# A two-layer hybrid-attention trunk on one core: projections in another order, roped tiles rounded later and a head at a time, one PSUM bank moved from projections to scores

## The chip, the cores and the metric

The kernel runs on one core of a Trainium2 chip. The metric is device time in microseconds for one launch; of the kernel before there are three timed runs, and one further execution was taken by the hardware profiler. Engine names are those of the profile: PE is TensorE, PEld its weight load, DVE VectorE, ACT ScalarE, POOL GpSimd, SP the queue that issues the DMAs.

## The reference

Two layers on `x` (1 x 512 x 1024, f32). Each layer has a mixer of three attention groups on one common projection, and a gated MLP with a causal depthwise convolution:

```python
for l in range(DEPTH):                       # 2
    h = rms_norm(x, attn_pre_norm[l])
    x = x + rms_norm(hybrid_mixer(h, ...), attn_post_norm[l])
    h = rms_norm(x, ffn_pre_norm[l])
    x = x + rms_norm(conv_ffn(h, ...), ffn_post_norm[l])
# hybrid_mixer: proj = h @ w_in, split into
(fq, fk, fv, ff, nq, kc, vc, ks, vs, kw, vw, ng, dq, dk, dv)
# o_fox: 4 heads, causal softmax with forget gates    (fq, fk, fv, ff)
# o_nsa: 8 heads in 2 groups, three branches summed with gates ng:
#        compressed (kc, vc), selected (ks, vs), sliding window (kw, vw)
# o_dil: 4 heads, dilated windows                      (dq, dk, dv)
# rope on nq, kc, ks, kw, dq, dk;   mix = concat(o_fox, o_nsa, o_dil) @ w_out
```

All matrices are f32. The kernel computes each product from parts in a rounded format: a value is rounded (its high part), the difference is rounded again (its low part), and high x high, high x low and low x high are summed.

## The kernel before, in words

A layer goes through these stages: the norm and its transposes, the projections fk, fv and fq, the *mixer* with all remaining projections, the end of the out projection, the norm, the up projection with convolution and gate, the down projection. The mixer of layer 0 lies at about 60 to 345 us of the span, that of layer 1 about 696 us later.

The mixer is a software pipeline of 96 *units*: one unit is one head, one branch and one of four query tiles of 128 rows (forget heads: units 0 to 15; NSA heads with the selected and the window branch: 16 to 79; dilated heads: 80 to 95). One unit starts in each *slot* of the loop, and `LAGS` says how many slots later its further stages follow: scores on PE (`st_scores`, lag 0), mask and maximum on DVE (`st_max`, 1), exponential on ACT (`st_exp`, 1), reciprocal on DVE and scaling on POOL (`st_norm`, 2), transposes on PE (`st_turn`, 4), rounding of the transposed tile on ACT and DVE (`st_keep_hi`, `st_keep_lo`, 5), products with v on PE (`st_values`, 7), evacuation (`st_out`, 7).

Between the slots `main_pieces` supplies the projections, cut into *steps* of about 1.4 us of PE: first five steps, then 1.4 steps in each of twelve slots, 0.8 after that. A projection of 128 columns (`projT`) takes four steps and ends in one PSUM bank of the pool `acc`; sv and dv (`proj256`) take eight steps and two banks. After its last step `keep` follows: the rope (`rope`: shuffle and cosine product on DVE, sine product and sum on POOL), and one step later `keep2`, the rounding of the roped tile, both heads of 64 rows in a row, in `q_evac` or `k_evac` (high part on ACT, low part on DVE; for k each of them twice, once for each half of the partitions). Before a unit's scores, `operands` looks whether its q, k and v are there; where not, `until` runs steps back to back until they are:

```python
def until(key, n=1):
    while len(store.get(key, ())) < n and (live[0] or pieces.late):
        step()
```

On PE this order of calls is the order of the program (`tc.manual_schedule`). On DVE, ACT and POOL a scheduler orders the instructions by their dependences and priorities. A list `plan` holds the weights in the order in which SP loads them; each is split into a high part (ACT, line 144) and a low part (POOL, line 148, for the names in `ONPOOL`; DVE, line 152, for others).

PSUM has eight banks, shared out by `PSB`: three for projections (`acc`), two for scores (`s`), two for transposes (`pt`), one for the products with v (`o`). A tile of a pool waits until the readers of the tile that had its bank are done. The compressed branch (`c_scores`, `c_norm`, `c_turn`, `c_keep`) runs beside units 47 to 57; its tiles are taken from the pool named by `CT`.

Of the kernel before, what the change touches and what calls it, by code (L numbers as in the profile page):

```python
# [13 lines left out]
ALU = mybir.AluOpType  # L14
# [11 lines left out]
NBIG = 24  # L26
NROW = 10
LAGS = (1, 2, 4, 5, 7, 7)
TAIL = 4
ONPOOL = ("sv", "dv", "dq", "dk", "ks", "nq0", "kw", "kc", "nq1",  # L30
          (0, "fk", 0), (0, "fk", 1), ("up", 0, 1), ("up", 0, 2), ("up", 0, 3), ("up", 1, 0))
# [3 lines left out]
CL = (1, 3, 5, 6)  # L35
OT = (("acc", "acc"), ("acc", "s"), ("s", "o"), ("acc", "acc"))
PCUT = ((0, 2), (2, 4))
X8 = "acc"
CT = "acc"
FIRST = 5  # L40
DCUTS = ("w1", "wo")
EV = (1, 3, 1, 1)
ORDER = (0, 1, 2, 4, 3, 5, 6, 7, 8)
# [29 lines left out]
def tile_hybrid_block(  # L73
# [15 lines left out]
    dram = ctx.enter_context(tc.tile_pool(name="dram", bufs=1, space=bass.MemoryType.DRAM))  # L89
    PSB = {"acc": 3, "o": 1, "s": 2, "pt": 2}  # L90
    uid = [0]
# [5 lines left out]
    def ps(tag):  # L97
        return psum.tile([128, 512], F32, tag=tag, bufs=PSB[tag], name=nm(tag))

    def bt(shape, dt=F32, name="b"):  # L100
        return big.tile(shape, dt, tag="b", name=nm(name))
# [7 lines left out]
    def f(ap):  # L109
        return ap.bitcast(F32)  # L110
# [50 lines left out]
    for l in range(DEPTH):  # L161
# [7 lines left out]
        def turned(name, *starts, spare=False):  # L169
            for c, c0 in enumerate(starts):  # L170
                plan.append(((l, name, c), [(wi[:, :, c0:c0 + 128], 0, 0)], 8, 128, spare))
# [6 lines left out]
        turned("kc", C_KC, C_KC + 128)  # L178
        turned("ks", C_KC + 256)
        for c in range(2):  # L180
            ks = slice(4 * c, 4 * c + 4)
            plan.append(((l, "sv", c), [(wi[:, ks, C_KC + 384:C_KC + 512], 0, 0), (wi[:, ks, C_KW + 128:C_KW + 256], 0, 128)],
                         4, 256, False))
        turned("nq0", C_NQ, C_NQ + 128)
        for kv, starts in enumerate(((C_KW,), (C_NQ + 256, C_NQ + 384))):
            for c in range(2):
                if c < len(starts):
                    plan.append(((l, ("kw", "nq1")[kv], c), [(wi[:, :, starts[c]:starts[c] + 128], 0, 0)], 8, 128, False))
                for d in range(2):
                    k0 = 8 * c + 4 * d  # L190
                    plan.append(((l, "w1", kv, 2 * c + d), [(w1s[kv][:, k0:k0 + 4, :], 0, 0)], 4, 256, False))
# [247 lines left out]
    for l in range(DEPTH):  # L439
# [21 lines left out]
        def rope(p):  # L461
# [6 lines left out]
            return r  # L468

        def q_evac(p):  # L470
            q = bt([128, 2, 512], F32R, "q")
            for j in range(2):
                src = p[64 * j:64 * j + 64, :]
                nc.scalar.activation(q[0:64, j, :], src, AF.Copy, scale=-0.125)
                nc.vector.scalar_tensor_tensor(q[64:128, j, :], src, -0.125, f(q[0:64, j, :]),  # L475
                                               op0=ALU.mult, op1=ALU.subtract)
            return q

        def k_evac(p):

            ks = []
            for j in range(2):
                k = bt([128, 2, 512], F32R, "k")
                src = p[64 * j:64 * j + 64, :]
                for u in (j, 1 - j):
                    nc.scalar.activation(k[64 * u:64 * u + 64, 0, :], src, AF.Copy)
                for u in (j, 1 - j):
                    nc.vector.tensor_sub(k[64 * u:64 * u + 64, 1, :], src, f(k[64 * j:64 * j + 64, 0, :]))  # L488
                ks.append(k)
            return ks  # L490
# [20 lines left out]
        wv = [getw(l, "fv", c, ahead=1) for c in range(3)]  # L511
        pk_ = [ps("acc"), ps("acc")]
        fv = [new_v(), new_v()]
# [205 lines left out]
        def keep(p, key):  # L719
            pieces.later(EV[3], keep2, rope(p), key)  # L720

        def keep2(r, key):
            store.setdefault(key, []).extend([q_evac(r)] if key[-1] == "q" else k_evac(r))

# [16 lines left out]
        def main_pieces():  # L741
# [69 lines left out]
            yield from projT("kc", turn=(win_k, win_v))  # L811
            yield from projT("ks", "nks")
            yield from proj256("sv", sv_evac, [])
            yield from projT("nq0", "nq")
            xc = rt((128, 256))
            for kv, g in ((0, projT("kw", "nkw")), (1, projT("nq1", "nq"))):
                while len(wins.get(kv, ())) < 2:
                    yield
                yield from merge(g, hidden(kv))
# [22 lines left out]
            yield from out_first()  # L842
            yield from out_start()

        def merge(a, b):
# [343 lines left out]
        with tc.manual_schedule(engines={mybir.EngineType.PE}):  # L1189
# [44 lines left out]
            table(AF.Silu, hs[3][:, 0:1])  # L1234
            pts = [ps(t) for t in ("acc", "acc", "s", "s")]
            for half in range(2):
# [17 lines left out]
        for i in range(11):  # L1254
            gt = bt([128, 2, 512], name="g")
            gts.append(gt)
            tg = ("acc", "acc", "s", "s") if i % 2 == 0 else ("pt", "pt", X8, "o")
            for c in range(2):
# [13 lines left out]

        dacc = [(ps("acc"), ps("acc")), (ps("s"), ps("s")), (ps("o"), ps(X8)), (ps("pt"), ps("pt"))]
        NK = DFF // 128
# [70 lines left out]
```

## Time and profile before

| | |
|---|---|
| timed runs, median (lowest to highest) | 1412.58 us (1411.82 to 1418.45) |
| profiled execution | 1416.81 us |
| its span (first to last instruction) | 1415.0 us, mean granted PE clock 0.986 |
| PE busy | 1337.1 us, 94% |
| DVE busy | 892.9 us, 63% |
| ACT busy | 725.6 us, 51% |
| POOL busy | 377.6 us, 27% |

A row of a timeline gives the start and the duration of an instruction (or of a run of equal ones, x count), its engine, line, operation, what it writes and reads, and in brackets how long the engine stood idle before it and which instruction ended that. The granted clock is a share of full speed; the two levels are 1.2 and 2.4 GHz, so that a mean between 0.5 and 1 is a stretch with both.

### The profile page before, as it was taken

How to read it: one execution, taken by the hardware profiler on the slowest of the kernel's cores; microseconds unless marked ns; L12 is line 12 of the kernel's file. 1: busy time of each engine (PE TensorE's matmuls, PEld its weight loads, DVE VectorE, ACT ScalarE, POOL GpSimd, SP SyncE). 2: the span in 40 equal slices, each digit the busy share in tenths (PEclk: the TensorE clock that was granted, in tenths of full speed). 3: DMA queues.
4: the chain of work that ended last, by engine and by line, in shares of the span. 5: the costliest groups of instructions: out<-in, count | busy, mean ns of one | idle time of the engine just before them, and what ended most of it. 6: DMA issues, size and time to landing. Idle time of an engine off the chain costs nothing.

```text
span 1415.0 us, 19975 instructions
## 1 busy us (share of the span) xinstructions
PE 1337.1 (94%) x7291; PEld 1151.2 (81%) x7291; DVE 892.9 (63%) x1867; ACT 725.6 (51%) x1469; POOL 377.6 (27%) x409
## 2 busy tenths in 40 slices
PE   6987999998999999999999988989989999999997
PEld 5876887887888888888887878979878888888886
DVE  7767878877655555533476687787686555554334
ACT  5656675775543333332374667677754333333322
POOL 2385576545000000000006657654440000000000
PEclk9999999999999999999999989999999999999999
DMA  6222321123233333323423132202313333323231
GB/s 175 76 60 75 99 71 31 46 75 119 66 99 96 98 96 98 96 98 111 119 90 90 60 105 75 60 31 69 112 60 89 91 103 91 103 91 104 90 120 59
DMA packets 161962, 123.67 MB, mean 87 GB/s; under 512 B 8329, under 2 KB 152137, under 8 KB 161865
## 3 DMA queue, kind: packets, MB, share of 16 engines
q1 hardware_dynamic: 161864, 122.40, 28.8%
q8 instruction: 57, 0.93, 0.3%
q14 instruction: 41, 0.33, 0.1%
HBM read 118.19 MB, written 4.19 MB: 86 GB/s over the span
## 4 chain that ended last, share of the span: by engine, by line
PE 70%; DVE 12%; ACT 7%; POOL 6%; issue 3%; DMA 1%; SPq 0%; POOLq 0%; DVEq 0%; ACTq 0%
PE acc L113 31%; PE s L113 16%; PE pt L113 12%; PE o L113 9%; PE pt L1107 2%; DVE k L488 1%; POOL r L467 1%; DVE q L475 1%; DVE wl_w L152 1%; POOL r L466 1%; ACT r L1089 1%; POOL wt L781 1%; DVE x L308 1%; DVE hl L274 1%; DVE pl L1129 1%
## 5 line engine op out<-in xcount | busy, mean ns | idle before, releaser
L152 DVE TENSOR_TENSOR wl_up<-raw_up,wh_up 128x1024 fp32r<-128x1024 f32 x78 | 95.5, 1225 | 163.2 <-ACT wh_up L144 163.2
L144 ACT ACTIVATE wh_up<-raw_up 128x1024 fp32r<-128x1024 f32 (+1 forms) x90 | 89.4, 1002 | 154.1 <-PE acc L113 67.9
L152 DVE TENSOR_TENSOR wl_wd<-raw_wd,wh_wd 128x1024 fp32r<-128x1024 f32 x42 | 51.5, 1225 | 133.5 <-ACT wh_wd L144 133.5
L113 PE MATMUL s<-k,q 128*128 128x512 f32 (+3 forms) x384 | 100.6, 343 | 23.8 <-DVE sm L1084 8.3
L148 POOL TENSOR_TENSOR wl_kc<-raw_kc,wh_kc 128x512 fp32r<-128x512 f32 x8 | 12.2, 1546 | 411.1 <-ACT wh_kc L144 411.1
L144 ACT ACTIVATE wh_wd<-raw_wd 128x1024 fp32r<-128x1024 f32 x42 | 44.5, 1060 | 144.5 <-PE pt L113 135.5
L1089 ACT ACTIVATE r<-r,sm 128x128 f32<-128x128 f32 x192 | 106.8, 557 | 19.7 <-DVE sm L1084 18.8
L1096 POOL TENSOR_SCALAR r<-r,sm,gates 128x128 f32<-128x128 f32 (+3 forms) x128 | 86.2, 680 | 88.0 <-DVE sm L1094 48.1
L113 PE MATMUL acc<-hh,wh_up 128*128 128x512 f32 (+1 forms) x272 | 102.4, 376 | 0.0
L113 PE MATMUL acc<-hl,wh_up 128*128 128x512 f32 (+1 forms) x272 | 102.4, 376 | 0.0
L113 PE MATMUL acc<-hh,wl_up 128*128 128x512 f32 (+1 forms) x272 | 102.4, 376 | 0.0
L113 PEld LDWEIGHTS s<-k,q 128*128 128x128 f32 x384 | 65.0, 198 | 36.0 <-DVE sm L1084 11.8
L1129 DVE TENSOR_TENSOR pl<-pt,ph 128x384 fp32r<-128x384 f32 x144 | 85.2, 593 | 13.0 <-ACT ph L1124 11.9
L1124 ACT ACTIVATE ph<-pt 128x384 fp32r<-128x384 f32 x144 | 74.4, 518 | 34.9 <-PE pt L1107 33.8
L1107 PE MATMUL pt<-ident,r 128*128 128x128 f32 x480 | 80.1, 283 | 7.7 <-POOL r L1096 4.9
L1084 DVE CUSTOM_DVE_ANT_0 r<-s,cmask 128x128 f32<-128x128 f32 (+3 forms) x160 | 74.8, 481 | 17.4 <-PE s L113 15.3
L113 PE MATMUL acc<-wh_wd,gh 128*128 128x512 f32 x252 | 83.7, 389 | 0.0
L113 PE MATMUL s<-hh,wh_up 128*128 128x512 f32 (+1 forms) x224 | 80.6, 360 | 0.9 <-DVE hl L274 0.9
L113 PE MATMUL s<-hl,wh_up 128*128 128x512 f32 (+1 forms) x224 | 80.3, 359 | 0.0
L113 PE MATMUL s<-hh,wl_up 128*128 128x512 f32 (+1 forms) x224 | 80.3, 359 | 0.0
L113 PE MATMUL o<-ph,v 128*128 128x256 f32 (+1 forms) x288 | 72.8, 279 | 0.8 <-DVE mx L1165 0.8
L113 PE MATMUL o<-pl,v 128*128 128x256 f32 (+1 forms) x288 | 70.0, 290 | 1.7 <-DVE pl L1129 1.7
(434 smaller groups left out, 4023.4 us busy)
## 6 DMA issues: line engine op xcount, KB each, us to landing
raw_up<-in_w_up_dram SPq DMA_DIRECT2D x88, 512.0 KB, 3.8
raw_wd<-in_w_down_dram SPq DMA_DIRECT2D x44, 512.0 KB, 3.4
raw_wo<-in_w_out_dram SPq DMA_DIRECT2D x16, 512.0 KB, 3.5
x<-in_x_dram SPq DMA_DIRECT2D x8, 512.0 KB, 5.7
raw_nq<-in_w_in_dram SPq DMA_DIRECT2D x8, 512.0 KB, 3.8
raw_w<-in_cmp_w_k_dram SPq DMA_DIRECT2D x8, 512.0 KB, 4.0
raw_w<-in_cmp_w_v_dram SPq DMA_DIRECT2D x8, 512.0 KB, 3.8
raw_fk<-in_w_in_dram SPq DMA_DIRECT2D x4, 512.0 KB, 4.8
```

What stands on the lines that cost most here:

```text
L113: nc.tensor.matmul(o, lhsT=lhsT, rhs=rhs, start=start, stop=stop, skip_group_check=True)
L144: nc.scalar.activation(hi[:, ks], raw[:, ks], AF.Copy)
L152: nc.vector.tensor_sub(lo[:, ks], raw[:, ks], f(hi)[:, ks])
L274: nc.vector.scalar_tensor_tensor(lo, src, gain[:, k:k + 1], f(hi), op0=ALU.mult, op1=ALU.subtract)
L308: nc.vector.scalar_tensor_tensor(xs[s][:, cs], hs[s][:, cs], stats["r", s // 2][:, j:j + 1], xs[s][:, cs], op0=ALU.mult, op1=ALU.add)
L466: nc.gpsimd.tensor_mul(w, w, sinT)
L1084: nc.vector.tensor_tensor_reduce(row[:, 0:n], u["S"][:, 0:n], u["mask"][:, 512 - n:512], op0=ALU.add, op1=ALU.min, scale=1.0, scalar=3.0e3 ...
L1089: nc.scalar.activation(row[:, 0:n], row[:, 0:n], AF.Exp, scale=-1.0, bias=sm_[:, 0:1], accum_out=sm_[:, 1:2])
L1096: nc.gpsimd.tensor_scalar(row[:, 0:n], row[:, 0:n], sm_[:, 2:3], g_, op0=ALU.mult, op1=ALU.mult)
L1107: nc.tensor.transpose(p[:, 128 * b:128 * b + 128], src, ident)
L1124: nc.scalar.activation(hi, src, AF.Copy)
L1129: nc.vector.tensor_sub(*u["lo"])
```

## The change

1. The order of the projections in `main_pieces`, and of the loads in `plan`. Before: kc, ks, sv, nq0 (two column groups), then kw merged with the first hidden layer of the compressed k, nq1 (two groups) merged with that of the compressed v, dv, dq, dk. After: kc, ks, nq0 (one group: heads 0 to 3's first 128 columns), kw, sv, then nq1 merged with the first hidden layer, nq2 and nq3 merged with the second, dv, dq, dk. The names nq0 to nq3 now stand for one group of 128 columns each.
2. `keep` does the rope at once, as before; the rounding of the two heads of a tile is now in two calls, two and three steps after the rope (`EV[3]` 1 to 2), instead of one call one step after it.
3. `PSB`: `acc` from three banks to two, `s` from two to three. Tiles that go from `acc` to `s`: the second of the two fk tiles, those of the compressed branch (`CT`), one of the out projection (`OT`), and one each in the transposes of the second norm, the up and the down projection.
4. `NROW` from 10 to 12: two more tiles of 128x512 f32 for rows.

The arithmetic is the same.

```diff
-NROW = 10
+NROW = 12
-ONPOOL = ("sv", "dv", "dq", "dk", "ks", "nq0", "kw", "kc", "nq1",
+ONPOOL = ("sv", "dv", "dq", "dk", "ks", "nq0", "kw", "kc", "nq1", "nq2", "nq3",
-OT = (("acc", "acc"), ("acc", "s"), ("s", "o"), ("acc", "acc"))
+OT = (("acc", "acc"), ("s", "s"), ("s", "o"), ("acc", "acc"))
-CT = "acc"
+CT = "s"
-EV = (1, 3, 1, 1)
+EV = (1, 3, 1, 2)
-    PSB = {"acc": 3, "o": 1, "s": 2, "pt": 2}
+    PSB = {"acc": 2, "o": 1, "s": 3, "pt": 2}
...
-        pk_ = [ps("acc"), ps("acc")]
+        pk_ = [ps("acc"), ps("s")]
...
         def keep(p, key):
-            pieces.later(EV[3], keep2, rope(p), key)
-
-        def keep2(r, key):
-            store.setdefault(key, []).extend([q_evac(r)] if key[-1] == "q" else k_evac(r))
+            r = rope(p)
+            if key[-1] == "q":
+                q = bt([128, 2, 512], F32R, "q")
+                pieces.later(EV[3], q_half, q, r, 0)
+                pieces.later(EV[3] + 1, last_q, key, q, r)
+            else:
+                pieces.later(EV[3], one_k, key, r, 0)
+                pieces.later(EV[3] + 1, one_k, key, r, 1)
+
+        def last_q(key, q, r):
+            q_half(q, r, 1)
+            store.setdefault(key, []).append(q)
+
+        def one_k(key, r, j):
+            k = bt([128, 2, 512], F32R, "k")
+            k_half(k, r, j)
+            store.setdefault(key, []).append(k)
...
             yield from projT("ks", "nks")
+            yield from projT("nq0", "nq")
+            yield from projT("kw", "nkw")
             yield from proj256("sv", sv_evac, [])
-            yield from projT("nq0", "nq")
             xc = rt((128, 256))
-            for kv, g in ((0, projT("kw", "nkw")), (1, projT("nq1", "nq"))):
+            for kv, g in ((0, projT("nq1", "nq")), (1, both(projT("nq2", "nq"), projT("nq3", "nq")))):
...
-            pts = [ps(t) for t in ("acc", "acc", "s", "s")]
+            pts = [ps(t) for t in ("acc", "s", "s", "s")]
...
-            tg = ("acc", "acc", "s", "s") if i % 2 == 0 else ("pt", "pt", X8, "o")
+            tg = ("acc", "s", "s", "s") if i % 2 == 0 else ("pt", "pt", X8, "o")
...
-        dacc = [(ps("acc"), ps("acc")), (ps("s"), ps("s")), (ps("o"), ps(X8)), (ps("pt"), ps("pt"))]
+        dacc = [(ps("acc"), ps("acc")), (ps("s"), ps("s")), (ps("o"), ps("s")), (ps("pt"), ps("pt"))]
```

`q_half` and `k_half` hold the loop bodies of the former `q_evac` and `k_evac`.

How the change moves instructions is seen at three places of layer 0. The first is PE ahead of the first score of slot 20, the first one that reads the window branch's k (`k_1577`); `acc_1510` is the compressed branch's first hidden layer with its weights `wh_w`, `wl_w`. Before:

```order
L113 MATMUL acc_1510<-wh_w_0_2_274_1541,wth_949 128x256 [waits Activation_49]
L113 MATMUL acc_1510<-wl_w_0_2_275_1542,wth_949 128x256 [waits DVE_49]
L113 MATMUL acc_1510<-wh_w_0_2_274_1541,wth_949 128x256
L113 MATMUL acc_1510<-wl_w_0_2_275_1542,wth_949 128x256
L113 MATMUL s_1587<-k_1577,q_1385 128x128 [waits Activation_49]
L113 MATMUL s_1587<-k_1577,q_1385 128x128 [waits DVE_49]
```

After, the same score (`k_1271` is now the window branch's k), and what stands before it:

```order
L113 MATMUL acc_1423<-hh_98,wh_nq_0_240_1346 128x512
L113 MATMUL acc_1423<-hl_102,wh_nq_0_240_1346 128x512
L113 MATMUL acc_1423<-hh_98,wl_nq_0_241_1347 128x512
L113 MATMUL s_1544<-k_1271,q_1104 128x128 x2
L113 MATMUL o_1555<-ph_1488,v_305 128x256 [waits DVE_49]
```

The score no longer carries a wait for ACT and DVE, and a step of nq1 (`wh_nq`) stands before it instead of the hidden layer.

The second is DVE's order around the rounding of the window branch's k: shuffle (line 464) and cosine product of the rope, then the low parts (line 488). Before:

```order
L464 STREAM_SHUFFLE r_1555<-acc_1468 128x512
L465 TENSOR_TENSOR r_1556<-acc_1468,cosT 128x512
L152 TENSOR_TENSOR wl_w_0_3_280_1564<-raw_w_0_3_273_1539,wh_w_0_3_279_1563 128x512 x2
L1084 ISA r_1591,sm_1592<-s_1481,cmask 128x512
L1084 ISA sm_1592 128x1
L488 TENSOR_TENSOR k_1577<-r_1556,k_1577 64x512 x2
L488 TENSOR_TENSOR k_1582<-r_1556,k_1582 64x512 x2
```

After, the rope and the first half; the second half (`k_1320`) stands 15 rows further on:

```order
L465 STREAM_SHUFFLE r_1211<-acc_1091 128x512
L466 TENSOR_TENSOR r_1212<-acc_1091,cosT 128x512
L1107 ISA r_1222,sm_1223<-s_1170,cmask 128x512
L1107 ISA sm_1223 128x1
L1152 TENSOR_TENSOR pl_1175<-pt_1184,ph_1174 128x4x128
L1117 RECIPROCAL sm_1223<-sm_1223 128x1
L483 TENSOR_TENSOR k_1271<-r_1212,k_1271 64x512 x2
```

Four low parts in a row became two and two, and maxima, low parts of transposed tiles and reciprocals stand between rope and rounding.

The third is PE at the start of the mixer: the cumulative sum of the forget gates (`utri`, tile `acc_722`), which follows the two projections of fq (`acc_654`, `acc_692`) and is followed by kc (`acc_795`). Before:

```order
L113 MATMUL acc_722<-utri,lfh_636 4x128 [waits DVE_49,PE_49]
L113 MATMUL acc_722<-utri,lfh_636 4x384
L113 MATMUL acc_722<-utri,lfl_637 4x128 [waits DVE_49]
L113 MATMUL acc_722<-utri,lfl_637 4x384
```

After:

```order
L113 MATMUL acc_722<-utri,lfh_636 4x128 [waits DVE_49,PE_49]
L113 MATMUL acc_722<-utri,lfh_636 4x384
L113 MATMUL acc_722<-utri,lfl_637 4x128
L113 MATMUL acc_722<-utri,lfl_637 4x384
```

The wait of its third row is gone because the first row now waits for a later instruction of DVE: with two banks `acc_722` takes the one of `acc_654`, whose last reader is the rounding of the first q, and `acc_795` takes that of `acc_692`.

## Rows read from the trace of the kernel before

**Rows 1.** The page: busy time of each engine (share of the span, instructions), and the chain that ended last, by engine.

```profile
PE 1337.1 (94%) x7291; PEld 1151.2 (81%) x7291; DVE 892.9 (63%) x1867; ACT 725.6 (51%) x1469; POOL 377.6 (27%) x409
...
PE 70%; DVE 12%; ACT 7%; POOL 6%; issue 3%; DMA 1%; SPq 0%; POOLq 0%; DVEq 0%; ACTq 0%
```

**Rows 2.** Whom PE waited for from 56 to 330 us (layer 0's mixer): engine, tile and line that waited, what it waited for, us in total, times, longest.

```profile
PE s L113 <- DVE sm L1084: 4.2, 4, 1.5
PE s L113 <- ACT k L486: 3.4, 1, 3.4
PE acc L1004 <- DVE sm L1094: 3.4, 1, 3.4
...
PE s L113 <- DVE k L488: 2.3, 1, 2.3
...
PE s L113 <- DVE q L475: 2.1, 1, 2.1
...
PE acc L113 <- DVE q L475: 1.1, 1, 1.1
```

**Rows 3.** PE's timeline in layer 0, the rows before which it stood idle.

```profile
60.88 0.47 PE L113 MATMUL acc<-hh,wh_kc 128*128 128x512 f32 x1 [1.07 <-DVE q L475]
...
87.26 0.55 PE L1107 MATMUL pt<-ident,r 128*128 128x128 f32 x3 [2.28 <-POOL r L1096]
...
119.91 0.44 PE L113 MATMUL s<-k,q 128*128 128x128 f32 x2 [2.05 <-DVE q L475]
...
138.51 0.33 PE L113 MATMUL s<-k,q 128*128 128x128 f32 x1 [3.42 <-ACT k L486]
...
141.09 0.48 PE L113 MATMUL s<-k,q 128*128 128x128 f32 x1 [2.25 <-DVE k L488]
...
165.51 0.73 PE L113 MATMUL s<-k,q 128*128 128x512 f32 x2 [1.50 <-DVE sm L1084]
...
183.91 0.73 PE L113 MATMUL s<-k,q 128*128 128x512 f32 x2 [1.10 <-DVE sm L1084]
185.38 0.63 PE L1107 MATMUL pt<-ident,r 128*128 128x128 f32 x4 [0.74 <-DVE sm L1094]
...
228.11 0.41 PE L1004 MATMUL acc<-ident,r 128*128 128x128 f32 x2 [3.36 <-DVE sm L1094]
...
302.69 0.50 PE L113 MATMUL pt<-pch,vcm 64*128 64x512 f32 x1 [1.23 <-DVE pl L1129]
```

**Rows 4.** PE's timeline in layer 1: the first matmul of kc, and three of the long waits.

```profile
755.45 0.47 PE L113 MATMUL acc<-hh,wh_kc 128*128 128x512 f32 x1
...
834.55 0.33 PE L113 MATMUL s<-k,q 128*128 128x128 f32 x1 [3.30 <-ACT k L486]
837.13 0.47 PE L113 MATMUL s<-k,q 128*128 128x128 f32 x1 [2.25 <-DVE k L488]
...
924.31 0.41 PE L1004 MATMUL acc<-ident,r 128*128 128x128 f32 x2 [3.36 <-DVE sm L1094]
```

**Rows 5.** Stretches of layer 0: from and to, length, then busy time (instructions) of PE, PEld, DVE, ACT and POOL, granted PE clock, share of the DMA engines, GB/s.

```profile
113.80:156.40 42.60, 34.87 (x199) 30.90 (x198) 33.74 (x79) 27.89 (x64) 24.41 (x23) 0.92 0.30 87
156.40:228.10 71.70, 64.62 (x459) 58.89 (x458) 57.48 (x172) 47.54 (x125) 50.84 (x62) 1.00 0.25 69
...
136.00:140.00 4.00, 0.33 (x1) 0.19 (x1) 3.99 (x6) 2.73 (x5) 4.00 (x3) 1.00 0.38 106
140.00:144.00 4.00, 2.91 (x13) 2.91 (x14) 3.72 (x9) 2.01 (x5) 1.61 (x2) 0.52 0.77 224
144.00:148.00 4.00, 4.00 (x22) 3.92 (x21) 2.93 (x6) 2.74 (x8) 1.36 (x2) 0.63 0.29 76
...
228.00:232.00 4.00, 3.89 (x14) 3.24 (x15) 3.82 (x13) 2.71 (x7) 1.60 (x3) 0.61 0.00 0
...
304.00:308.00 4.00, 4.00 (x23) 4.00 (x22) 2.41 (x11) 2.15 (x8) 3.17 (x5) 0.57 0.77 250
```

**Rows 6.** ACT, DVE and POOL around the rounding of kw before slot 20, and last DVE at fk in layer 1.

```profile
137.18 2.59 ACT L486 ACTIVATE k<-r 64x512 fp32r<-64x512 f32 x4 [1.92 <-POOL r L467]
...
134.59 3.10 DVE L152 TENSOR_TENSOR wl_w<-raw_w,wh_w 128x512 fp32r<-128x512 f32 x2
...
138.22 4.24 DVE L488 TENSOR_TENSOR k<-r,k 64x512 fp32r<-64x512 f32 x4
...
137.11 3.38 POOL L148 TENSOR_TENSOR wl_nq<-raw_nq,wh_nq 128x512 fp32r<-128x512 f32 x2
...
741.33 1.40 DVE L488 TENSOR_TENSOR k<-acc,k 64x512 fp32r<-64x512 f32 x2 [0.23 <-ACT k L486]
```

**Rows 7.** DVE's roundings of q at the start of the mixer, in layer 0 (the last of the first tile, the last of the second) and in layer 1 (the last of the second).

```profile
60.03 0.69 DVE L475 SCALAR_TENSOR_TENSOR q<-acc,q 64x512 fp32r<-64x512 f32 x1 [0.66 <-ACT q L474]
...
62.52 0.70 DVE L475 SCALAR_TENSOR_TENSOR q<-acc,q 64x512 fp32r<-64x512 f32 x1 [0.66 <-ACT q L474]
...
757.09 0.69 DVE L475 SCALAR_TENSOR_TENSOR q<-acc,q 64x512 fp32r<-64x512 f32 x1 [0.66 <-ACT q L474]
```

**Rows 8.** ACT and DVE before the transposes of the compressed branch at 228.11.

```profile
224.81 1.28 ACT L474 ACTIVATE q<-r 64x512 fp32r<-64x512 f32 x2 [1.33 <-POOL r L467]
...
226.11 1.40 DVE L475 SCALAR_TENSOR_TENSOR q<-r,q 64x512 fp32r<-64x512 f32 x2
```

**Rows 9.** One of DVE's subtractions that empty a tile of v (layer 1, fv).

```profile
744.02 0.29 DVE L498 TENSOR_TENSOR v<-s,v 128x128 fp32r<-128x128 f32 x1
```

More of the change, by code (lines that the diff above doesn't have):

```diff
@@ L179, in tile_hybrid_block @@
         turned("ks", C_KC + 256)
+        turned("nq0", C_NQ)
+        turned("kw", C_KW)
         for c in range(2):
@@ L183, in tile_hybrid_block @@
                          4, 256, False))
-        turned("nq0", C_NQ, C_NQ + 128)
-        for kv, starts in enumerate(((C_KW,), (C_NQ + 256, C_NQ + 384))):
+        for kv in range(2):
             for c in range(2):
-                if c < len(starts):
-                    plan.append(((l, ("kw", "nq1")[kv], c), [(wi[:, :, starts[c]:starts[c] + 128], 0, 0)], 8, 128, False))
+                if kv or c == 0:
+                    turned("nq%d" % (1 + kv + c), C_NQ + 128 * (1 + kv + c))
                 for d in range(2):
@@ L468, in rope, with q_half, k_half @@
             return r
+        def q_half(q, p, j):
+            src = p[64 * j:64 * j + 64, :]
+            nc.scalar.activation(q[0:64, j, :], src, AF.Copy, scale=-0.125)
+            nc.vector.scalar_tensor_tensor(q[64:128, j, :], src, -0.125, f(q[0:64, j, :]),
+                                           op0=ALU.mult, op1=ALU.subtract)
+        def k_half(k, p, j):
+            src = p[64 * j:64 * j + 64, :]
+            for u in (j, 1 - j):
+                nc.scalar.activation(k[64 * u:64 * u + 64, 0, :], src, AF.Copy)
+            for u in (j, 1 - j):
+                nc.vector.tensor_sub(k[64 * u:64 * u + 64, 1, :], src, f(k[64 * j:64 * j + 64, 0, :]))
         def q_evac(p):
@@ L472, in q_evac @@
             for j in range(2):
[L473 to L476, printed above, removed]
+                q_half(q, p, j)
             return q
         def k_evac(p):
-            ks = []
+            ks = [bt([128, 2, 512], F32R, "k") for j in range(2)]
             for j in range(2):
[L483 to L489, printed above, removed]
+                k_half(ks[j], p, j)
             return ks
@@ L843, in main_pieces, with both @@
             yield from out_start()
+        def both(a, b):
+            yield from a
+            yield from b
         def merge(a, b):
```

## The prediction

> **What bounds the kernel now.** I read the page first, then who waited for whom on PE, then PE's timeline at each wait, and last the clock and the busy times by stage. TensorE is busy for 1337.1 us of the span and makes 70% of the chain that ended last; no other engine is over 63% [rows 1]. So time can only come out of PE's idle time and of the stretches at a lower clock. In the mixer of layer 0 (about 56 to 330 us) the named waits are few and long: scores behind the maximum of an earlier tile 4.2 us, behind the rounding of k 3.4 and 2.3, behind q 2.1, and the transposes of the compressed branch 3.4 [rows 2]. The timeline puts them at slots: 2.05 us at 119.91 (slot 16, first NSA head), 3.42 and 2.25 at 138.51 and 141.09 (slot 20, first window branch), 3.36 at 228.11, and score waits of 1.50, 1.10 and (via the reciprocal) 0.74 at 165.51, 183.91 and 185.38 [rows 3]. Layer 1 has the same ones within 0.12 us [rows 4]. After two of them the granted clock is down: 0.52 and 0.63 in the 8 us from 140, 0.61 in the 4 us from 228, between 1.2 and 2.4 GHz as a mean over each [rows 5]. The FFN and the out projection are not touched beyond the banks that tiles rotate through, and I count them at nothing, since a matmul there has its operands and a free bank long before its turn; that cover would be gone if a bank were still being read when its turn came.
>
> **The change, part by part, for one layer.**
>
> *Order and split halves.* Slot 16 waits for the last q rounding and slot 20 for the rounding of kw because the loop forces the missing pieces out just before the scores that need them, and the rope (at slot 20 ACT waits 1.92 us for POOL's last addition) and the roundings follow on the spot [rows 6]. Now nq0 and kw are projected several slots earlier, and their halves lie in other slots, so these scores find their operands. Removed: 2.05 + 3.42 + 2.25 = 7.7 us of idle, and the low clock behind it, 4 × 0.48 + 4 × 0.37 = 3.4 us; 11.1 at most. But the stretch cannot shrink by that much. It lasts 42.6 us from 113.8 to 156.4, and DVE works 33.7 of them [rows 5]: 8.9 us is the end on that side. The other end is nothing, if the same DVE work only gets a new place to be waited for. I take 6, a stretch of 36.6 us. At that length DVE would be 92% busy with its present durations. These should fall: the four k subtractions took 1.06 us each and two splits 1.55 each while POOL worked beside them, against 0.70 for one alone [rows 6]; 4 × 0.36 us off leaves 32.3, 88%. The next stretch, 71.7 us without a long wait, shows DVE at 80% and PE at 90%, so 88% is already demanding, and I go no lower [rows 5]. The forced burst does not vanish: it now stands before slot 16 and consists of the second half of sv, 48 matmuls of 256 columns, and one piece of nq1. PE works through it, and nothing in it is an operand of the scores that follow.
>
> *A third bank for scores.* Of the waits for the maximum, 1.50 + 1.10 + 0.74 = 3.3 us can go [rows 3]; I take 1.5, since the chain of maximum, exponential, scaling and transpose behind a score tile is as long as before and some waits will only move to the transposes. Ends: 0 and 3.3. The earlier ones count for nothing: at 87.26 PE waits 2.28 us for POOL, which is late whatever scores do before [rows 3].
>
> *The compressed branch in the score banks.* The wait of 3.36 us is behind two roundings of q of 0.70 each, which stand ahead of the subtraction that frees the bank [rows 8], and behind the rope that ACT waits for. One rounding now stands there. With its clock (4 × 0.39 = 1.6 us [rows 5]) at most 4.9 us go. Against that the branch's score and transpose tiles now share three banks with the ordinary scores for some fourteen slots: two or three waits of the size of those above, 0.74 to 1.50 us [rows 3], could appear, 3 us at the other end. I take +2.5.
>
> *Two accumulation banks: the start.* This is a loss that can be read off. Before, the first matmul of kc waited 1.07 us for the first q of fq and began at 60.88 [rows 3]. With two banks the small cumulative-sum tile takes that bank, and kc has to wait for the second q, whose last rounding ends at 62.52 + 0.70 = 63.22 [rows 7]; with the 0.16 us from release to start seen before (60.72 to 60.88), kc starts at 63.4, 2.5 us later. In layer 1 the same sum is 757.09 + 0.69 + 0.16 = 757.94 against 755.45, 2.5 us again [rows 4, 7]. The rope of kc and POOL's chain to 87.26 hang on it, so I see nothing that hides it: −2.5. If POOL had slack there it would be 0; the wait at 87.26 says that it has none.
>
> *Two accumulation banks: later.* sv fills both banks, so the next projection begins only when eight subtractions have emptied them, 8 × 0.29 = 2.3 us at most behind the burst [rows 9]. nq2, nq3 and dv follow each other with the rope of the one before still reading. Between 0 and −3; I take −1.
>
> *Two more row tiles* and the later weight splits cost nothing: the rows only loosen, and POOL has the same number of splits to make, hidden under PE; without that cover each would show as a wait of PE for a weight, and there is none in the list [rows 2].
>
> Sum per layer: 6 + 1.5 + 2.5 − 2.5 − 1 = 6.5 us, 13 for two. All of it is against the profiled execution, 1416.8 us with a span of 1415.0, which gives 1403.8. That execution lies 4.2 us above the median of the runs; the same 13 us off 1412.6 give 1399.6, and I say 1400. With every best end, 8.9 + 3.3 + 4.9 − 2.5 = 14.6 per layer, 1383; with every worst, 0 + 0 − 3 − 2.5 − 3 = −8.5, 1430.
>
> **A rule on the clock.** PE idled 1.50, 1.10 and 0.74 us between 156.4 and 228.1 and the granted clock of that stretch stayed at 1.00; it fell after 3.42 + 2.25 and after 3.36 us, but also in the 4 us from 304, to 0.57, after a wait of only 1.23 at 302.69 [rows 3, 5]. The Trainium skill (TensorE: Matmul & The Clock Gate, "A second HAM failure mode: psum-queue depth-cycling") says that short idle moments between groups of matmuls, as PE cycles through PSUM banks, can be frequent enough to swing the clock between its two levels. By that rule fewer accumulation banks would cost clock besides idle time; the stretch at 1.00 speaks against it, the place at 304 for it.
>
> **Rivals.**
> 1. *The waits move.* DVE sets the length of 113.8 to 156.4 after all and the gain of the order is 2 instead of 6; the rest as above gives 2.5 per layer, 1407.6. For it: DVE at 3.7 to 4.0 of 4 us around the long wait [rows 5]. Against it: it was slower there per instruction than elsewhere.
> 2. *Slower: the banks decide.* With two accumulation banks each projection has to wait until the rope of the one before the last has read its tile, and with the compressed branch in the score banks a score waits for its subtraction. Price: 2.5 at the start, 3 later, 3 in the compressed branch, 8.5 per layer; it decides once the order gains less than that. With the order at 3 and 0 for the third bank, −5.5 per layer: 1423.6. For it: bank waits are already the largest group [rows 2]. Against it: they are on score tiles, and the only wait of a projection for a bank in layer 0 is the 1.07 us at the start.
> 3. *Clock.* The gain in idle time comes, but four of the new short waits per layer each bring a stretch like that from 228, 1.6 us: 6.4 per layer, and the time is 1412.4. The rule above is this mechanism.
> 4. *More goes*: the best ends of order and compressed branch, about 11 per layer, 1390.6. For it: both lost clock stretches stood behind the waits that go.
>
> **Chances.** Forecast (about 1395 to 1407) 0.47, rival 1 0.17, rival 2 0.16, rival 3 0.07, rival 4 0.13. About 0.5%, 7 us, is what a measurement here can tell from no change: 1405.5 to 1419.6. Nearly all of the forecast's share, its last piece above 1405.5 left out, and all of rival 4 are faster: 0.58. Rivals 1 and 3 and the rest of the forecast make no difference: 0.27. Rival 2, with a piece of it inside the bound, is slower: 0.15. The range for 8 in 10 leaves out the far half of rival 2 and the best ends: 1387 to 1417. The likeliest case alone is 1395 to 1407.
>
> **What would show it.** Right: no wait of PE for k or q at slots 16 and 20; clock 1.00 from there on; first matmul of kc near 63.4 with a wait for a q rounding, and at 757.9 in layer 1; scores with hardly a wait for the maximum outside the compressed branch. Wrong: the last score of slot 27 no earlier against that start than now, the transposes of the compressed branch still 3 us late, or waits on projection tiles adding up to more than 6 us per layer. A kc that starts at 61 would show that the loss at the start is not real.

## The result: slower by 1.2%

The changed kernel takes 1433.16 us (median of 4 runs, 1432.36 to 1434.22) against 1415.51 for the kernel before in the same count of runs; the ratio is 1.0123, with an interval of 1.0097 to 1.0148. The forecast was 1400, the range ended at 1417. The profiled execution took 1432.9 us, its span is 1431.1 us. The kernel before spreads more, from 1411.8 to 1418.7 us over all its runs, and its profiled execution, 1416.8, lies in the upper part, so that comparisons of profiles with it show some us too little of a loss.

The page of after, the rows that answer to [rows 1]:

```profile
span 1431.1 us, 19945 instructions
...
PE 1341.8 (94%) x7291; PEld 1154.1 (81%) x7291; DVE 894.6 (63%) x1867; ACT 726.5 (51%) x1469; POOL 385.6 (27%) x409
...
PE 65%; DVE 13%; ACT 8%; POOL 8%; issue 4%; DMA 1%; SPq 0%; ACTq 0%; DVEq 0%; POOLq 0%
```

The span is 16.1 us longer than that of the profile before. PE's busy time has grown by 4.7 us with the same 7291 matmuls, which goes with a mean granted clock of 0.980 instead of 0.986, and its idle time by the rest, from 77.9 to 89.3 us (span less busy). Whom PE waited for, from 56 to 340 us of after (layer 0's mixer, engine, tile and line, what it waited for, us, times, longest):

```profile
PE pt L1130 <- POOL r L1119: 10.7, 6, 4.3
PE pt L1130 <- DVE sm L1117: 5.0, 2, 3.4
PE acc L113 <- DVE v L503: 3.1, 1, 3.1
PE acc L113 <- DVE q L474: 2.9, 2, 2.7
PE s L1027 <- DVE pcl L1035: 1.9, 1, 1.9
PE acc L113 <- DVE r L466: 1.8, 2, 1.0
```

All that headed the list before is gone: no score waits for a maximum, for k or for q [rows 2]. In its place, transposes wait for POOL's scaling (L1119, before L1096) and for the reciprocal ahead of it, and projections wait for a bank. PE's timeline in after shows where:

```profile
61.10 0.59 PE L113 MATMUL acc<-utri,lfh 128*4 128x128 f32 x2 [2.66 <-DVE q L474]
63.58 0.77 PE L113 MATMUL acc<-hh,wh_kc 128*128 128x512 f32 x1 [0.19 <-DVE q L474]
...
91.84 0.90 PE L1130 MATMUL pt<-ident,r 128*128 128x128 f32 x3 [3.80 <-POOL r L1119]
...
112.32 1.09 PE L1130 MATMUL pt<-ident,r 128*128 128x128 f32 x4 [3.41 <-DVE sm L1117]
...
133.27 0.77 PE L113 MATMUL acc<-hh,wh_nq 128*128 128x512 f32 x1 [3.07 <-DVE v L503]
...
197.72 0.90 PE L1130 MATMUL pt<-ident,r 128*128 128x128 f32 x3 [4.26 <-POOL r L1119]
...
241.38 0.41 PE L1027 MATMUL s<-ident,r 128*128 128x128 f32 x2 [1.92 <-DVE pcl L1035]
```

These rows answer to [rows 3]. In this execution the clock is down behind each of the waits of 2.66 us and more (0.63 in the 4 us from 92 and 0.57 in those from 112, beside the rows below). Stretches of after (from and to, length, busy time of PE, PEld, DVE, ACT, POOL, then the granted clock, the share of the DMA engines, GB/s), to be held against [rows 5]:

```profile
60.00:64.00 4.00, 2.71 (x15) 1.93 (x16) 2.22 (x5) 3.02 (x6) 2.58 (x3) 0.60 0.51 131
64.00:68.00 4.00, 4.00 (x11) 3.09 (x11) 0.68 (x1) 0.01 (x1) 0.00 (x0) 0.55 0.51 131
...
132.00:136.00 4.00, 2.73 (x7) 2.18 (x8) 2.76 (x8) 2.37 (x8) 0.16 (x1) 0.56 0.36 119
136.00:140.00 4.00, 4.00 (x17) 3.50 (x16) 0.00 (x0) 0.00 (x0) 0.00 (x0) 0.59 0.53 131
196.00:200.00 4.00, 2.28 (x11) 2.28 (x12) 3.18 (x10) 2.23 (x7) 3.13 (x5) 0.67 0.41 113
...
123.15:161.36 38.21, 32.97 (x210) 29.54 (x208) 29.63 (x79) 27.21 (x70) 16.33 (x18) 0.91 0.27 74
161.36:231.87 70.51, 64.48 (x459) 60.00 (x458) 53.48 (x167) 46.01 (x124) 50.12 (x59) 0.98 0.26 75
```

The last two rows run from slot 15 to 27 and from 27 to 55, as the first two of [rows 5] do: 38.2 against 42.6 us and 70.5 against 71.7. So the stretch that the forecast was about did get shorter, by 4.4 us; but slot 15 itself starts at 123.15 instead of 113.80, 9.3 us late. Counted from the first matmul of kc (63.58 against 60.88), slot 27 begins after 97.8 us instead of 95.5: up to there nothing has been gained. After slot 55 more is lost; the transposes of the norm behind the mixer begin at 352.72 instead of 342.40.

### The profile page after: what moved, and what is told of

Its sections match the earlier page's. It is cut to its first block, busy times and chain, and to the rows that moved or that the text cites. A ratio compares the mean times of both kernels' runs of the same rounds, so it can differ in the third digit from the quotient of the medians.

```text
span 1431.1 us, 19945 instructions
## 1 busy us (share of the span) xinstructions
PE 1341.8 (94%) x7291; PEld 1154.1 (81%) x7291; DVE 894.6 (63%) x1867; ACT 726.5 (51%) x1469; POOL 385.6 (27%) x409
## 4 chain that ended last, share of the span: by engine, by line
PE 65%; DVE 13%; ACT 8%; POOL 8%; issue 4%; DMA 1%; SPq 0%; ACTq 0%; DVEq 0%; POOLq 0%
PE s L113 22%; PE acc L113 21%; PE pt L113 12%; PE o L113 8%; PE pt L1130 2%; POOL r L468 2%; ACT r L1112 2%; DVE pl L1152 1%; DVE r L1107 1%; POOL r L467 1%; DVE k L483 1%; POOL wt L799 1%; DVE x L309 1%; POOL r L1119 1%; DVE q L474 1%
## 5 line engine op out<-in xcount | busy, mean ns | idle before, releaser
L1119 POOL TENSOR_SCALAR r<-r,sm,gates 128x128 f32<-128x128 f32 (+3 forms) x128 | 94.8, 746 | 99.6 <-DVE sm L1117 66.7
L113 PE MATMUL s<-hh,wh_up 128*128 128x512 f32 (+1 forms) x336 | 121.0, 360 | 0.4 <-DVE hl L275 0.4
L113 PE MATMUL s<-hl,wh_up 128*128 128x512 f32 (+1 forms) x336 | 120.6, 359 | 0.0
L113 PE MATMUL s<-hh,wl_up 128*128 128x512 f32 (+1 forms) x336 | 120.6, 359 | 0.0
L113 PE MATMUL s<-k,q 128*128 128x512 f32 (+3 forms) x384 | 96.8, 334 | 1.0 <-DVE pcl L1035 1.0
L1130 PEld LDWEIGHTS pt<-ident,r 128*128 128x128 f32 x480 | 56.3, 144 | 44.5 <-POOL r L1119 25.6
L113 PE MATMUL s<-wh_wd,gh 128*128 128x512 f32 x252 | 83.9, 390 | 0.0
L113 PEld LDWEIGHTS s<-hh,wh_up 128*128 128x128 f32 x336 | 63.7, 189 | 10.2 <-issue 0.6
L113 PEld LDWEIGHTS s<-hl,wh_up 128*128 128x128 f32 x336 | 63.6, 189 | 9.5
L113 PEld LDWEIGHTS s<-hh,wl_up 128*128 128x128 f32 x336 | 63.6, 189 | 9.3
```

The costliest lines, as they stand in the source:

```text
L113: nc.tensor.matmul(o, lhsT=lhsT, rhs=rhs, start=start, stop=stop, skip_group_check=True)
L1119: nc.gpsimd.tensor_scalar(row[:, 0:n], row[:, 0:n], sm_[:, 2:3], g_, op0=ALU.mult, op1=ALU.mult)
L1130: nc.tensor.transpose(p[:, 128 * b:128 * b + 128], src, ident)
```

## The experiments

The change has three parts that can be taken apart: the order, the split and later rounding (with the 12 row tiles), and the banks. Two theories stood against each other at first: that the two projection banks cost the time, and that the order does, by putting the ropes of nq0 and kw where POOL is full. Below stand medians, and their ratios to the kernel before as measured on the same chip, with 95% intervals; differences between two changed kernels are differences of medians.

**One part alone on the kernel before.** `b_banks`:

```diff
-    PSB = {"acc": 3, "o": 1, "s": 2, "pt": 2}
+    PSB = {"acc": 2, "o": 1, "s": 3, "pt": 2}
```

and the tiles that go with it (`CT`, `OT`, `pk_`, `pts`, `tg`, `dacc`).

> The kernel before with the banks alone (two for projections, three for scores, the tiles that go with them). Theory banks (the two banks are where the time went: kc held at the start, the projection after sv held, each with a stretch at a lower clock behind it): slower by 5 to 15 us, 1420 to 1430, with waits of PE on projection tiles of over 5 us per layer. Theory order (the time went with nq0 and kw pulled into the stretch where POOL is full): no slower than before, 1405 to 1416, since the score waits of 8.3 us and the compressed branch's 6.7 us mostly go.

Measured 1421.0 us, 1.0052 (1.0033 to 1.0072). The time is the one expected, but its waits on projection tiles are 3.8 us in layer 0 and 2.3 in layer 1, not over 5, and a part of what the third score bank takes away only moves. Whom PE waited for from 56 to 350 us in `b_banks`:

```profile
PE pt L1107 <- POOL r L1096: 4.4, 2, 3.7
PE acc L113 <- DVE q L475: 3.8, 2, 2.7
PE pt L1107 <- DVE sm L1094: 3.7, 2, 2.1
```

The first line was 2.5 us in all before, with 2.28 at 87.26 as the longest [rows 3]. Before that wait the kernel before had two score waits, which are gone here:

```profile
75.87 0.74 PE L113 MATMUL s<-k,q 128*128 128x512 f32 x2 [0.78 <-DVE sm L1084]
78.99 0.44 PE L113 MATMUL s<-k,q 128*128 128x128 f32 x2 [0.77 <-DVE sm L1084]
```

Their 1.55 us stand before the transposes instead. `b_order`, the lists in `plan` and `main_pieces` and `ONPOOL` alone:

> The kernel before with the order alone (nq0, kw before sv; three banks for projections, rounding one step after the rope). Theory order: slower than before, 1422 to 1432, with waits of transposes for POOL of 8 us or more per layer. Theory banks: faster than before by 8 to 14 us, 1401 to 1407, as the waits at slots 16 and 20 go and no bank is short.

Measured 1435.66 us, 1.0148 (1.0121 to 1.0175): 22 us, more than the whole change and more than this theory said; the transposes wait 10.4 us for POOL in layer 0. `b_halves`, `keep` with two calls, `EV[3]` 2, `NROW` 12:

> The kernel before with the rounding split and later (two and three steps after the rope) and 12 row tiles, the rest as before. Theories banks and order: little, within 6 us of before, since the forced steps at slots 16 and 20 only get longer by one step. Theory halves (the later rounding is what costs, as it stands ahead of maxima in DVE's queue): 1422 or more.

Measured 1419.8 us, 1.0037 (1.0025 to 1.0049). So each part is a loss by itself, and 22 + 7 + 6 = 35 us together, nearly twice what they cost in one kernel: they are not independent.

**Two parts together.** `a_oldbanks` is the change without the banks, `a_oldkeep` without the later rounding, `a_oldorder` without the order.

> The changed kernel with the banks of before (three for projections, two for scores): order and split rounding together. If the bank move costs here what it cost alone (7 us): 1426. If the third score bank repays in the new order, where the order alone left 9.8 us of score waits and a 4.8 us wait of the compressed branch per layer: 1436 to 1442, slower than the changed kernel.

Measured 1418.74 us, 1.0038 (1.0023 to 1.0053): 14.4 us faster than the changed kernel, outside both expectations.

> The changed kernel with the rounding of a tile in one call, one step after the rope, as before: order and banks together. If the split rounding costs here what it cost alone (6 us): 1427. If it lightens what the order does to DVE's queue: 1436 or more.

Measured 1447.04 us, 1.0242 (1.0226 to 1.0258), as the second case said.

> The changed kernel with the order of before: banks and split rounding together. If banks and rounding only add: 1427. If the two banks cost more beside the later rounding, since a rope read late holds one of two banks, as they do beside the new order (14.5 us there against 7): 1430 or more. If the third score bank takes away what the late rounding costs alone: 1422 or less.

Measured 1426.4 us, 1.0093 (1.0071 to 1.0116), the sum of the two parts. With these the eight combinations are complete (us; the kernel before in its runs beside them 1413.7; the kernels at 1413.7, 1421.0 and 1435.7 have 10 row tiles, the other five 12):

| | old banks | new banks |
|---|---|---|
| old order, old rounding | 1413.7 | 1421.0 |
| old order, late halves | 1419.8 | 1426.4 |
| new order, old rounding | 1435.7 | 1447.0 |
| new order, late halves | 1418.7 | 1433.2 |

Read along the rows, the banks cost 7, 7, 11 and 14 us: always a loss, and the largest one in the kernel as changed. Read down with the old banks, the order costs 22 with the early rounding and gains 1 with the late one; with the new banks, as in the change, it costs 26 and 7.

**Why the order needs the late rounding.** `b_order` shows one hold at the first q of NSA. POOL, ACT, DVE and PE (for each its own row of the timeline):

```profile
103.76 1.26 POOL L468 TENSOR_TENSOR r<-r,r 128x512 f32<-128x512 f32 x1
...
105.06 1.28 ACT L475 ACTIVATE q<-r 64x512 fp32r<-64x512 f32 x2 [5.24 <-POOL r L468]
...
105.72 0.68 DVE L476 SCALAR_TENSOR_TENSOR q<-r,q 64x512 fp32r<-64x512 f32 x1 [5.51 <-ACT q L475]
106.43 0.29 DVE L1090 CUSTOM_DVE_ANT_0 r<-s,cmask 128x128 f32<-128x128 f32 x1
...
107.95 0.73 PE L113 MATMUL s<-k,q 128*128 128x512 f32 x2 [4.11 <-DVE sm L1090]
```

The rounding stands at the head of DVE's queue for 5.5 us, because ACT's part waits for the rope's sum, which POOL does between splits of sv; the maxima stand behind it, and the next score has no bank. Is it the lateness that helps, or the split into two calls? `o_late` rounds whole, three steps after the rope, `o_split` in halves, one and two steps after it; both have the new order, the old banks and 12 row tiles. `b_order` has 10, so that against it both also show what two more row tiles are worth; `o_split` differs from `a_oldbanks` in `EV[3]` alone, 1 for 2.

```diff
-EV = (1, 3, 1, 1)
+EV = (1, 3, 1, 3)
```

> The new order with the old banks and 12 row tiles, the rounding in one call but three steps after the rope. Theory lateness: the rounding no longer heads DVE's queue while the rope is on POOL, and the time is near that of late and split, 1417 to 1424, with the 5.5 us in which DVE waits for ACT at the first q of NSA cut to 3 or less. Theory split: as the order alone, 1432 to 1437.

Measured 1419.34 us, 1.0031 (1.0017 to 1.0044), the same as late and split. The hold at the same place in `o_late`, on DVE:

```profile
104.69 1.75 DVE L476 SCALAR_TENSOR_TENSOR q<-r,q 64x512 fp32r<-64x512 f32 x1 [3.93 <-ACT q L475]
```

It is shorter by 1.6 us, not below 3 as expected; the same row stands in after at 109.28. PE gains nothing there, since two score waits in `o_late` add up to more than the 4.11 us above:

```profile
98.90 0.62 PE L113 MATMUL s<-k,q 128*128 128x384 f32 x2 [0.99 <-DVE sm L1090]
107.17 1.22 PE L113 MATMUL s<-k,q 128*128 128x512 f32 x2 [3.48 <-DVE sm L1090]
```

The first transposes of the compressed branch come no earlier either, at 228.36 against 227.69. The gain of this layer, 8.0 us at the norm behind the mixer (345.77 against 353.73), arises behind them. The compressed branch's transposes wait 2.8 us instead of 4.8, and this score of `b_order`, for whose bank a maximum stood behind roundings of a k in DVE's queue, has a short wait in `o_late`, as have the transposes behind it (first `b_order`, then `o_late`):

```profile
263.35 1.22 PE L113 MATMUL s<-k,q 128*128 128x512 f32 x2 [3.68 <-DVE sm L1090]
```

```profile
258.41 0.74 PE L113 MATMUL s<-k,q 128*128 128x512 f32 x2 [0.63 <-DVE sm L1090]
259.80 0.63 PE L1113 MATMUL pt<-ident,r 128*128 128x128 f32 x4 [0.66 <-DVE sm L1100]
```

> The new order with the old banks and 12 row tiles, the rounding in two calls, one and two steps after the rope. Theory lateness: the first half still waits at the head of DVE's queue, 1428 to 1436. Theory split: 1417 to 1424.

Measured 1426.75 us, 1.0077 (1.0051 to 1.0102), between the two theories. Against `b_order` the split with the row tiles gives 9 us, the lateness with the row tiles 16; what the row tiles give of each was not run. Shown with all else equal are 8 us for one step of lateness on top of the split (1418.74 against 1426.75), and 14 us for lateness and split together on the new banks (1433.16 against 1447.04).

**Where the banks cost.** `a_pcs` moves one small tile of the changed kernel:

```diff
-        pcs = ps("acc")
+        pcs = ps("s")
```

> The changed kernel with one tile moved: the cumulative sum of the forget gates takes a score bank, so that kc need not wait for the second q. If only idle time counts, it gives back 1.6 to 1.8 us in layer 0 and 1.2 in layer 1: 1430. If the stretch at a lower clock behind the wait (0.60 and 0.55 in the 8 us from 60) is a part of the price, some 3 us more in layer 0: 1426 to 1428, and the clock of 60 to 68 us is 1.00.

Measured 1425.37 us, 1.0072 (1.0050 to 1.0095): 7.8 us faster than the changed kernel, more than either number expected. Its profile says where it comes from: PE idle 85.5 us (−3.8) and PE busy 1336.7 us (−5.1). At the start in `a_pcs`:

```profile
60.87 0.47 PE L113 MATMUL acc<-hh,wh_kc 128*128 128x512 f32 x1 [1.08 <-DVE q L474]
```

```profile
60.00:64.00 4.00, 3.13 (x14) 2.62 (x15) 2.90 (x6) 2.82 (x5) 2.54 (x2) 1.00 0.48 131
64.00:68.00 4.00, 4.00 (x19) 3.01 (x18) 1.33 (x3) 1.48 (x6) 0.85 (x1) 1.00 0.50 137
```

The kernel waits 1.08 us, as before, instead of 2.66, and the clock is 1.00. Not all of the gain belongs to the start. In layer 0 kc begins 2.7 us earlier, and 1.9 us more are won by the transposes at 87.24 (91.84 in after). Another 2.8 us are won behind the wait for sv, which is as long as in after (3.09 us, at 128.64), but here leaves the clock at 1.00, where after has 0.56 and 0.59:

```profile
128.64 0.47 PE L113 MATMUL acc<-hh,wh_nq 128*128 128x512 f32 x1 [3.09 <-DVE v L503]
```

```profile
128.00:132.00 4.00, 3.36 (x18) 2.92 (x19) 2.47 (x7) 2.09 (x7) 0.00 (x0) 1.00 0.41 130
132.00:136.00 4.00, 4.00 (x32) 3.82 (x31) 2.52 (x9) 2.98 (x8) 0.98 (x2) 1.00 0.38 111
```

So the length of a wait alone does not say whether slow matmuls follow it. `a_pcs_sv` does the same for one of the two tiles of sv as well:

```diff
-            pp = [ps("acc"), ps("acc")]
+            pp = [ps("acc"), ps("s" if name == "sv" else "acc")]
```

> The changed kernel with the cumulative sum and the second tile of sv in score banks. Theory banks (start and sv are the two places where the two projection banks cost): 1416 to 1420, about what the same kernel has with the three banks of before, 1418.7; the wait of 3.1 us at 133 is gone and so is the low clock behind it. If the wait only moves to the scores: 1423 to 1426.

Measured 1417.88 us, 1.0027 (1.0015 to 1.0040): another 7.5 us. nq1 then starts at 125.64 with no wait. With these two tiles moved the new banks are worth what the old ones are (1418.7): in the changed kernel the two places make up the whole net price of the banks.

**POOL's queue.** Ahead of the transposes at 197.72 in after POOL does this:

```profile
190.01 1.31 POOL L148 TENSOR_TENSOR wl_dq<-raw_dq,wh_dq 128x512 fp32r<-128x512 f32 x1
191.26 1.30 POOL L468 TENSOR_TENSOR r<-r,r 128x512 f32<-128x512 f32 x1
192.50 1.30 POOL L148 TENSOR_TENSOR wl_dq<-raw_dq,wh_dq 128x512 fp32r<-128x512 f32 x1
193.74 0.63 POOL L929 TENSOR_TENSOR r<-r 128x256 f32<-128x256 f32 x1
194.46 0.72 POOL L930 TENSOR_SCALAR r<-r 128x256 f32<-128x256 f32 x1
195.27 1.03 POOL L931 TENSOR_TENSOR r<-r,r 128x256 f32<-128x256 f32 x1
196.26 0.72 POOL L935 TENSOR_TENSOR r<-w2r,r 128x256 fp32r<-128x256 f32 x1
196.97 1.45 POOL L1119 TENSOR_SCALAR r<-r,sm,gates 128x384 f32<-128x384 f32 x2
```

The scaling in the last row could have begun at 190.6, when its reciprocal was done; it stands behind two splits, the rope of nq3 and the compressed branch's activation. In the four kernels of the table with the new order this wait is 4.3 to 5.2 us, in the four with the old order no wait from 170 to 200 us is over 2.1 us. Before, the same splits, rope and activation lay close together too, but scalings came between them (182.32, 184.09 and 187.51); that nq3's later place makes the difference is an argument, not a run. `a_dq` and `a_nqkw` take names out of `ONPOOL`, which gives these splits to DVE.

> The changed kernel with the weight splits of dq on DVE instead of POOL. Theory POOL's queue (the scaling that the transposes at 197.7 wait 4.3 us for stands ready at 190.6 behind splits of dq, the rope of nq3 and the compressed branch's products): two splits of 1.3 us leave the queue ahead of it, the wait falls to 1.7 us or less and the stretch at 0.67 behind it goes: 4 us per layer, 1424 to 1426. Theory dependence (the wait is the chain through the rope itself): 1431 to 1434.

Measured 1428.35 us, 1.0105 (1.0087 to 1.0123). The wait, at 194.08 there, is 1.33 us, but 2.09 us come anew at 198.62 for a product of the compressed branch on POOL (line 942), and the time lies between the two theories.

> The changed kernel with the weight splits of nq0 and kw on DVE instead of POOL. Theory POOL's queue: the wait of 3.8 us at 91.8 loses the 2 to 3.2 us of wl_kw ahead of the scaling, and what follows on POOL comes earlier: 1423 to 1428. If DVE's own queue sets the place: 1431 or more.

Measured 1427.43 us, 1.0099 (1.0083 to 1.0115). The wait of 3.80 us at 91.84 is 1.44 (at 88.56), that of 3.41 at 112.32 is 1.82. The first of the two is POOL's in either order: it is 2.28 us before, 2.30 in `b_order` and 2.31 in `a_oldbanks`, but 3.7 in `b_banks`, where splits of sv stand in the place of those of kw. The second comes with the order: near 108 to 114 us PE waits 3.4 to 4.1 us at once in `b_order`, `a_oldbanks`, `a_oldkeep` and after, and in none of the four kernels with the old order.

**A version from these.** Both arrangements of banks with the splits of nq0, kw and dq on DVE:

> The changed kernel with the banks of before and the splits of nq0, kw and dq on DVE. If the gains measured one by one add (14.5 for the banks, 5.8 and 4.9 for the splits): 1408, faster than before. If POOL's waits were hidden behind others in this arrangement: 1413 to 1419.

Measured 1410.76 us, 0.9973 (0.9962 to 0.9985), between the two expectations.

> The changed kernel with the cumulative sum and the second sv tile in score banks and the splits of nq0, kw and dq on DVE. If the gains add: 1406 to 1410. If one wait takes the place of another: 1412 to 1418.

Measured 1406.3 us, 0.9947 (0.9928 to 0.9966): faster than both kernels, by 7.4 us and by 27. Its page, and whom PE waited for from 56 to 350 us:

```profile
span 1403.8 us, 19936 instructions
...
PE 1330.4 (95%) x7291; PEld 1144.6 (82%) x7291; DVE 905.4 (64%) x1875; ACT 723.9 (52%) x1461; POOL 370.7 (26%) x393
```

```profile
PE pt L1130 <- POOL r L1119: 5.4, 6, 1.4
PE pt L1130 <- DVE sm L1117: 3.9, 2, 2.1
PE pt L269 <- DVE h L327: 2.6, 2, 2.2
```

PE's busy time is 11.4 us below that of the changed kernel and its idle time 73.4 us, 15.9 below. In this stretch no wait is longer than 2.2 us. Not tried: other places of nq3 in the order, the 12 row tiles alone, and splits on DVE in the kernel before. So it is not shown that the 7.4 us are owed to the new order; the transposes wait for POOL in the old order too, though less (2.5 us in layer 0 of the kernel before, 10.7 in after).

## Why the prediction was wrong

*What bounds the kernel* was right, and three of the signs came: no wait at slots 16 and 20, scores without waits, and kc at 63.58 where 63.4 was forecast. The fourth did not: the clock is 0.91 from slot 15 to 27 and 0.98 from there to 55, not 1.00. Two of the forecast's own marks of failure appeared: slot 27 is no earlier against the start of kc (97.8 against 95.5 us), and waits on projection tiles are more than 6 us per layer, 3.1 + 2.9 + 1.8 = 7.8. The third nearly did: the compressed branch's transposes wait 0.94 + 1.92 = 2.9 us.

*Order and split halves, forecast +6 per layer, 12 in all.* Measured without the banks: −5 (1418.7 against 1413.7); on the new banks −12 (1433.2 against 1421.0). The stretch from slot 15 to 27 did shrink, by 4.4 us with a new wait of 3.07 in it, and the scores found their operands. The step that failed: only this stretch was costed. The ropes, roundings and splits that left slots 15 to 20 had to be done elsewhere in the queues of POOL and DVE, and there they were put at nothing: "the later weight splits cost nothing", "hidden under PE". The runs show two places. Near 108 to 114 us the rounding of the first q stands in DVE's queue until POOL has its rope (held 3.93 us in after), and PE waits 3.41 us at 112.32; near 188 to 198 us a scaling stands behind splits, nq3's rope and the compressed branch, and PE waits 4.26 us at 197.72. That is 7.7 us, as much as the 2.05 + 3.42 + 2.25 that went. Moving the splits of nq0 and kw, and those of dq, off POOL gave 5.7 and 4.8 us, which shows that POOL's queue sets these waits; it also shortened the wait at 91.84, which is none of the order's. Rival 1, "the waits move", had the right mechanism but named DVE, and the stretch where they had been instead of those where they went.

*The split rounding* I treated with the order. The runs show that late and split it makes the order bearable (17 us on the old banks with the two row tiles, 14 on the new ones), that one step of lateness is worth 8 of these, and that on the old order it costs 6. Why it is worth so much is shown only in part: the named waits of layer 0 that it shortens lie behind 228 us.

*A third bank for scores and the compressed branch, forecast +1.5 and +2.5.* The score waits went as said, from 8.7 us in layer 0 of `a_oldbanks` to none. But with the two dear tiles moved the new banks are worth 0.9 us over the old ones (1417.9 against 1418.7), within what these runs can tell: the transposes wait instead. At the first of them it can be read off: 0.78 and 0.77 us of score waits go, and the wait for POOL grows from 2.28 to 3.80. The compressed branch's transposes wait 2.9 us where those of `a_oldbanks` wait 2.8. These 8 us of gain in two layers were not there. The prediction said that some waits will only move to the transposes; nearly all did.

*Two accumulation banks, forecast −2.5 and −1.* Here the mechanism and the start time were right and the size was not: moving the tile at the start gave 7.8 us where 5 were forecast, 2.8 of them clock behind the sv wait, and moving that of sv 7.5 where 2 were forecast for everything behind the start. For sv I had taken eight subtractions of 0.29 us as the upper end, 2.3 us, and 1 us as the value. They took longer: they stand behind a rounding of k (2.30 us) and splits in DVE's queue, and each waits for ACT's half, so that PE stood for 3.07 us. Two rows of DVE in after:

```profile
126.80 2.30 DVE L483 TENSOR_TENSOR k<-r,k 64x512 fp32r<-64x512 f32 x2 [0.30 <-ACT k L481]
...
131.56 0.29 DVE L503 TENSOR_TENSOR v<-acc,v 128x128 fp32r<-128x128 f32 x1 [0.27 <-ACT v L502]
```

*The clock*, last, is the common error. I put lost clock on the side of the gains, 3.4 and 1.6 us behind waits that go, and not on the side of the losses, though the one of 2.5 us that I forecast at the start was about as long as those that went. In after the 8 us from 60 have a clock of 0.60 and 0.55, and `a_pcs`, without that wait, has less busy time by 5.1 us and less idle time by 3.8. What stood in the prediction as rival 3, with 0.07, is a part of the losses. It can't be read from the length of a wait: 2.28 us at 87.26 before and 3.09 us at 128.64 in `a_pcs` left the clock at 1.00. The Trainium skill (TensorE: Matmul & The Clock Gate, "A second HAM failure mode: psum-queue depth-cycling") tells of a kernel in which PE, as it cycles through PSUM banks, idles briefly between groups of matmuls, often enough to swing the clock. What this case shows is clock lost behind single waits, 2.66 to 4.26 us long in after; no run here shows the case of that page.

Rival 2, "the banks decide", named the direction and two of the three places, at 1423.6; the measured time is worse still, since order and banks both lose: 14 us for the banks and 7 for the order in the changed kernel.

## What to carry to other kernels

Work that is pulled forward to save a wait has to be costed where it arrives: list every instruction of it on every in-order queue there, and ask what stands behind the one that waits longest. An instruction that is issued before its operand can be ready is dear on an engine that others wait for; with the rounding two and three steps after the rope instead of one, the same order cost nothing here on the old banks. And a long wait of PE has to be priced with slow matmuls behind it, on the side of the losses as on that of the gains, as a range: here some waits of 3 us had them and some had none.

## What was not expected of the hardware

In after a wait of 2.66 us at the start was followed by stretches of 4 us at 0.60 and 0.55, in `a_pcs` one of 1.08 us at the same place by none. Waits of the same length did not always bring a lower clock: 3.07 us at 133.27 in after did, 3.09 us at the same instruction in `a_pcs` did not. A rounding of q on DVE took 1.75 us at 104.69 in `o_late` against 0.69 for the next one at 107.69; POOL began a weight split (104.62, 1.27 us) just then.
